# Norm sums moved to the vector engine, a reordered head of each feed-forward block, and a second queue for the last transfers, in a two-layer encoder

## The chip, the cores and the metric

The program runs on one core of a Trainium2 chip. A core has a matrix engine (PE, with its weight loads shown as PEld), a vector engine (DVE), a scalar engine (ACT), a general engine (POOL) and a sync engine (SP) that issues transfers. Each engine takes its instructions strictly in the order in which they were written for it and waits at the head of its own queue. The metric is the device time of one execution in microseconds (us); lower is better.

## The reference

A hybrid encoder of two layers over two independent sequences (256 and 512 tokens, laid side by side as 768 columns), model width 1024. What matters here, cut from the reference:

```
for l in range(DEPTH):                      # 2 layers
    mod = silu(c) @ adaln_w[l] + adaln_b[l] # shift, scale, gate, twice
    h = rmsnorm(x, norm_g[l, 0]) * (1 + sc1) + sh1
    y = mlstm_mixer(h, ...) if l == 0 else swa_mixer(h, ...)   # both end in "@ w_out"
    x = x + g1 * y
    h = rmsnorm(x, norm_g[l, 1]) * (1 + sc2) + sh2
    x = x + g2 * conv_ffn(h, ...)           # h @ w_up, conv over tokens, silu(g)*val, @ w_down
return rmsnorm(x, final_g)                  # rmsnorm: x * rsqrt(mean(x*x) + EPS) * g
```

## The kernel before, in words

**Layout.** Activations lie as 8 chunks of 128 channels (KC = 8) by tokens. Every float32 product is made of three matmuls on a high and a low part of each operand ("whi" and "wlo" for weights, "yh/yl" and "zh/zl" for activations): the cast on ACT (L260) makes the high part, a subtraction on DVE (L261) the low part. Weight loads come through a ring of five buffers called raw (issued on SP, L269).

**Output projection (`out_proj`).** The tokens are treated as two halves of 384 columns. There are 16 tiles: 8 output chunks for the first half, then 8 for the second. Each tile is 24 matmuls of 128x384 into one of four PSUM banks, then DVE adds the result to x (`resid`, L590) and ACT squares x for the coming norm (`Norm.square`, L111). `Norm.square` also adds most squares into one running sum on DVE (L115). It is a generator: `head` below runs its last part.

**The norm (`Norm`).** The mean over channels is made on PE: each kept square tile is multiplied by a constant column (tiles "pa<-inv,nt"). With `on_pe=2` three tiles are kept (one running sum and two single squares), and there are three blocks of 128 tokens, so 9 products of width 2; each shows as 2 records. Then ACT adds epsilon (L150), POOL raises to the power -1/2 (L153), and PE spreads the factor over the partitions (tiles "pa<-kct,nr"). The generator `stages` yields between these steps; `apply` then multiplies and splits. The last norm of the program has `on_pe=KC` and starts its products early (`begin`, L129).

**The head of each feed-forward block (`head`).** Pairs of up-projection chunks are computed with a seven-product scheme on quarters of h: `outset` is the first two of a chunk's products (`quarters` on B11, then on B21, 12 matmuls each, on the first half of the tokens, whose norm is done). Meanwhile the second half's norm runs, and each `step()` advances it: it makes the operands T1, T2, T4, B22 and T3 from both halves. `sums(i)` makes, on DVE and one cast on ACT, the weight combinations of chunk i of the first pair out of its raw loads. Here PE, ACT and DVE run exactly in the written order (`manual_schedule`). `mark` writes a dummy matmul into a bank to claim it. The next pairs (`pair`) make their weight combinations on POOL (L1202, L1205, L1206); `issue_after` keeps the second pair behind instructions that `head` returns.

**The end.** The last norm's `apply` is `output`: ACT copies the spread factor from PSUM to SBUF (`side`, L574); per chunk of 128x256 either DVE multiplies straight from PSUM (L581), or ACT scales (L578) and POOL multiplies by `side` (L579); each chunk goes out by a transfer on SP (L582).

Of the kernel before, what the change touches and what calls it, by code (L numbers as in the profile page):

```python
# [11 lines left out]
F32 = mybir.dt.float32  # L12
# [4 lines left out]
P = 128  # L17
# [72 lines left out]
class Norm:  # L90
# [16 lines left out]
    def square(self, c):  # L107

        net = self.net
        sq = net.tmp([P, self.n])  # L110
        net.nc.scalar.activation(sq, self.x(c), AF.Square)  # L111
        self.sums.append(sq)
        if 2 <= len(self.sums) and self.count < KC - self.on_pe:
            acc = self.sums[0]
            self.adds.tensor_tensor(acc, acc, self.sums.pop(), ALU.add)  # L115
        self.count += 1
# [3 lines left out]
    def begin(self, n):  # L120

        if self.pm is None:
            self.pm = self.net.pa()
            self.sides = [self.pm[:, 2 * b : 2 * b + 2] for b in range(self.n // P)]
            self.done = 0
        for i in range(self.done, n):
            for b, o in enumerate(self.sides):

                self.net.nc.tensor.matmul(  # L129
                    o, self.sums[i][:, b * P : (b + 1) * P], self.net.inv,  # L130
                    start=i == b == 0, stop=i == KC - 1, skip_group_check=True,
                )
        self.done = max(self.done, n)

    def stages(self):
# [17 lines left out]
        nc.gpsimd.tensor_tensor(r, r, net.mhalf[:, :nb], ALU.pow)  # L153
        yield 2.0

        pr = net.pa()[:, : self.n]
        for b in range(nb):
            net.mm(pr[:, b * P : (b + 1) * P], r[:, b : b + 1].to_broadcast([P, P]), net.ident, True, True)
# [9 lines left out]
class Net:  # L168
# [402 lines left out]
    def output(self, x, pr, rng):  # L571
        nc = self.nc
        side = self.tmp([P, rng[1] - rng[0]])
        nc.scalar.copy(side, pr)  # L574
        for c in range(KC):

            if c in ((2, 5, 7), (0, 2))[rng is RANGES[1]]:
# [4 lines left out]
            self.nc.sync.dma_start(self.io["y"][:, c, rng[0] : rng[1]], x(c))  # L582
# [9 lines left out]
    def out_proj(self, u0, act, xt, l, apply):  # L592
# [16 lines left out]
        norms = [Norm(self, xt, half, apply, last=True, adds=self.nc.vector) for half in HALVES]  # L609
# [9 lines left out]
        for i, (z, c, w) in enumerate(todo):  # L619
            if i in (KC, 2 * KC - 1):  # L620
                yield
# [452 lines left out]
    def combined(self, l, i, pool):  # L1074
# [19 lines left out]

        def apply(x, pr, rng):
            if rng[0] == 0:
                for c in range(KC):
# [9 lines left out]
            dsh = pool.tile([P, 4], F32, name="dsh")  # L1107
            nc.vector.tensor_tensor(
                dsh, self.mod[l][:, 24 * i + 4 : 24 * i + 8, q], self.mod[l][:, 24 * i : 24 * i + 4, q], ALU.subtract
            )  # L1110
# [73 lines left out]
    def outset(self, o, w, r1):  # L1184
# [3 lines left out]
        self.quarters(o, part(0), self.B11, True)  # L1188
# [68 lines left out]
    def head(self, u0, last_tile, pool, urows, mark, early):  # L1257
# [18 lines left out]
        for t in banks[0][1:]:  # L1276
            mark(t)

        def sums(i):
# [4 lines left out]
            tt(s2, s1_, s2, ALU.subtract)  # L1284
            tt(s4, s4, s2, ALU.subtract)
            tt(s1[i][1], s1_, s1[i][0].bitcast(F32), ALU.subtract)
            tt(s1_, a22, s2, ALU.subtract)

# [9 lines left out]
        sums(0)  # L1298
        wc[0] = self.split(ra[0])
# [12 lines left out]
        pa = lambda: self.pa()[:, :H]  # L1312
        second = self.outset(pa(), wa[1], rows[1][0])
        next(second)
# [54 lines left out]
        return act.ins, dve.ins  # L1369
# [298 lines left out]
```

## Time and profile before

| | |
|---|---|
| runs | 1840.19 us median of 3 (1839.05 to 1841.2) |
| the profiled execution | 1839.38 us, its span 1837.3 us |
| granted PE clock over the span | 0.993 |
| PE busy | 1792.4 us (98%) |
| DVE, ACT, POOL busy | 1373.0 (75%), 893.9 (49%), 486.6 (26%) us |
| head of layer 0 and of layer 1 | about 500 to 550 us and 1285 to 1336 us |
| last norm's spread to the end of the span | 1829.1 to 1837.3 us |

How to read it: the span runs from the first to the last instruction of the program; the execution's time has some 2 us more around it. A row of a timeline gives the start, the duration, the engine, the line, the operation with output and inputs, how many were merged (x), and in brackets how long the engine had been idle before and what ended that. Matmuls overlap: the duration of one is longer than the distance to the next one's start, and it is the distance that counts when PE is full.

### The profile page before, as it was taken

What the parts mean: (1) busy time and instruction counts of PE and PEld (TensorE: products, weight loads), DVE (VectorE), ACT (ScalarE), POOL (GpSimd) and SP (SyncE); (2) the same over time, 40 slices, a digit from 0 to 9 for tenths busy, and PEclk for the clock granted to TensorE, in tenths of its full rate; (3) what the DMA queues carried; (4) which work ended last, traced back from release to release, by engine and by line L of the source; (5) the groups of instructions that cost most, each with busy time, mean ns of one, the idle gap of its engine ahead of it and who ended that gap; (6) DMA issues with size and microseconds to landing.
All of it is one profiled execution on the core that took longest, in us unless ns stands there. A gap on an engine that the chain in (4) does not pass through costs nothing.

```text
span 1837.3 us, 28927 instructions
## 1 busy us (share of the span) xinstructions
PE 1792.4 (98%) x11290; PEld 1657.9 (90%) x11290; DVE 1373.0 (75%) x2101; ACT 893.9 (49%) x1815; POOL 486.6 (26%) x386
## 2 busy tenths in 40 slices
PE   6999999999999999999999999999999999999997
PEld 3987887889998999999999999889889999999997
DVE  4755676886689877777777867766898777787876
ACT  4444443344456444444444557665464444444443
POOL 1001001031024333333331313320234333333322
PEclk9999999999999999999999999999999999999998
DMA  8344556546312212222222331234122222222212
GB/s 332 118 147 134 172 195 223 164 140 213 104 46 71 79 58 69 69 70 69 69 69 83 114 92 42 61 97 127 46 81 70 69 69 70 70 69 70 69 35 69
DMA packets 64245, 184.48 MB, mean 100 GB/s; under 512 B 6167, under 2 KB 23831, under 8 KB 64108
## 3 DMA queue, kind: packets, MB, share of 16 engines
q1 hardware_dynamic: 64108, 182.63, 30.7%
q8 instruction: 89, 1.46, 0.3%
q14 instruction: 48, 0.39, 0.1%
HBM read 176.17 MB, written 6.43 MB: 99 GB/s over the span
## 4 chain that ended last, share of the span: by engine, by line
PE 87%; DVE 5%; DMA 3%; ACT 2%; issue 1%; POOL 1%; SPq 0%; POOLq 0%; ACTq 0%; DVEq 0%
PE ps L254 29%; PE pa L254 24%; PE ps L1169 10%; PE ps L1172 10%; PE ps L1170 10%; PE pa L1008 1%; DMA slab<-in_adaln_w_dram 1%; DMA raw<-in_adaln_w_dram 1%; DMA raw<-in_w_dram 1%; DVE wlo L261 1%; DVE ada L506 1%; PE pa L1169 0%; PE pa L1172 0%; PE pa L1170 0%; DMA slab<-mrows 0%
## 5 line engine op out<-in xcount | busy, mean ns | idle before, releaser
L260 ACT CAST whi<-raw 128x1024 fp32r<-128x1024 f32 x237 | 247.9, 1048 | 344.2 <-PE pa L254 145.6
L261 DVE TENSOR_TENSOR wlo<-raw,whi 128x1024 fp32r<-128x1024 f32 x237 | 321.7, 1358 | 112.9 <-ACT whi L260 110.5
L254 PE MATMUL pa<-slab,whi 128*128 128x256 f32 (+1 forms) x1328 | 317.2, 334 | 0.0
L254 PEld LDWEIGHTS pa<-slab,whi 128*128 128x128 f32 x1328 | 230.2, 189 | 21.8 <-DVE slab L590 0.2
L590 DVE SCALAR_TENSOR_TENSOR slab<-pa,mod,slab 128x256 f32<-128x256 f32 (+1 forms) x332 | 192.8, 598 | 65.1 <-PE pa L254 65.0
L254 PE MATMUL pa<-slab,wlo 128*128 128x256 f32 (+1 forms) x664 | 212.7, 333 | 0.0
L254 PE MATMUL ps<-zh,whi 128*128 128x256 f32 (+1 forms) x560 | 189.2, 339 | 2.2 <-ACT whi L260 1.6
L254 PE MATMUL ps<-zh,wlo 128*128 128x256 f32 (+1 forms) x560 | 183.9, 330 | 1.7 <-DVE wlo L261 1.7
L254 PE MATMUL ps<-zl,whi 128*128 128x256 f32 (+1 forms) x560 | 185.0, 333 | 0.5 <-DVE zl L552 0.5
L1169 PE MATMUL ps<-zh,whi 128*128 128x384 f32 x504 | 172.2, 342 | 3.7 <-ACT nt L1240 1.9
L1170 PE MATMUL ps<-zl,whi 128*128 128x384 f32 x504 | 169.9, 337 | 1.8 <-DVE zl L1126 1.8
L1172 PE MATMUL ps<-zh,wlo 128*128 128x384 f32 x504 | 168.9, 335 | 0.0
L254 PE MATMUL ps<-slab,whi 128*128 128x384 f32 (+2 forms) x656 | 163.1, 332 | 0.9 <-DVE slab L261 0.5
L1205 POOL TENSOR_TENSOR raw<-raw,raw 128x512 f32<-128x512 f32 x40 | 52.0, 1299 | 331.0 <-DVE wlo L261 246.4
L254 PEld LDWEIGHTS pa<-slab,wlo 128*128 128x128 f32 x664 | 125.2, 189 | 12.6 <-DVE wlo L261 0.4
L1402 POOL TENSOR_TENSOR slab<-slab 128x772 f32<-128x772 f32 x44 | 86.5, 1968 | 166.0 <-DVE slab L1390 154.0
L1389 DVE SCALAR_TENSOR_TENSOR slab<-slab,cstt,slab 128x771 f32<-128x771 f32 x88 | 104.6, 1190 | 26.7 <-ACT slab L1387 26.5
L254 PEld LDWEIGHTS ps<-zh,whi 128*128 128x128 f32 x560 | 107.4, 192 | 15.8 <-issue 4.4
L506 DVE SCALAR_TENSOR_TENSOR ada<-raw,silc,ada 128x1024 f32<-128x1024 f32 x84 | 110.2, 1350 | 14.7 <-DMA raw<-in_adaln_w_dram 14.7
L254 PEld LDWEIGHTS ps<-zl,whi 128*128 128x128 f32 x560 | 107.4, 193 | 12.7 <-issue 3.4
L1202 POOL TENSOR_TENSOR raw<-raw 128x512 f32<-128x512 f32 x40 | 65.6, 1639 | 201.0 <-DMA raw<-in_w_dram 167.8
L254 PEld LDWEIGHTS ps<-slab,whi 128*128 128x128 f32 x656 | 115.1, 188 | 3.4 <-ACT whi L260 0.9
(291 smaller groups left out, 4336.7 us busy)
## 6 DMA issues: line engine op xcount, KB each, us to landing
raw<-in_w_dram SPq DMA_DIRECT2D x208, 512.0 KB, 3.7
raw<-in_adaln_w_dram SPq DMA_DIRECT2D x84, 512.0 KB, 4.6
slab<-in_x_dram SPq DMA_DIRECT2D x12, 512.0 KB, 7.9
slab<-in_adaln_w_dram SPq DMA_DIRECT2D x12, 512.0 KB, 10.2
slab<-mrows SPq DMA_DIRECT2D x8, 384.0 KB, 5.6
xs<-slab SPq DMA_DIRECT2D x6, 512.0 KB, 3.2
bt<-brow SPq DMA_DIRECT2D x16, 192.0 KB, 3.1
slab<-xs SPq DMA_DIRECT2D x6, 512.0 KB, 5.8
```

Source lines behind the costliest of these rows:

```text
L254: self.nc.tensor.matmul(out, lhsT, rhs, start=start, stop=stop)
L260: nc.scalar.copy(hi, src)
L261: return nc.vector.tensor_tensor(lo, src, hi.bitcast(F32), ALU.subtract)
L506: stt(acc[:, s], row, w, acc[:, s], ALU.mult, ALU.add)
L590: self.nc.vector.scalar_tensor_tensor(x, o, self.mod[l][:, gc + c, q : q + 1], x, ALU.mult, ALU.add)
L1169: mm(o, wh[:, k], hi[k], start=start and k == 0, stop=False, skip_group_check=True)
L1170: mm(o, wh[:, k], lo[k], start=False, stop=False, skip_group_check=True)
L1172: mm(o, wl[:, k], hi[k], start=False, stop=k == 3, skip_group_check=True)
L1202: tt(q[2], q[2], q[3], ALU.add)
L1205: tt(q[0], q[2], q[0], ALU.subtract)
L1389: stt(y[:, 1:], u[:, :-1], w(0), y[:, 1:], ALU.mult, ALU.add)
L1402: nc.gpsimd.tensor_tensor(y, y, yrow[:, j], ALU.mult)
```

## The change

It has these parts. (1) The two norms behind the output projection get `on_pe` 0 and 1 in place of 2: more squares are added on DVE, and fewer products of width 2 are made on PE. (2) `out_proj` hands over to `head` two tiles before its end in place of one, and stops inside these two tiles, so that `head` can place their residual, square and add between its own weight sums; `begin(1)` puts the first products of the second norm right behind the last tile. (3) In `head`, the low-part matmuls of a first block stand at its end (`low`), and the norm's next step runs ahead of them; the second chunk's first block comes between the first chunk's two; chunk 1's weight cast comes behind the epsilon. (4) `head` returns the power instruction too, and the second pair's POOL work is kept behind it. (5) A small subtraction (`dsh`) moves to the first half's `apply`. (6) At the end the factor is spread twice, into two PSUM tiles (`twin`), ACT reads the second; two chunks in place of three go over ACT and POOL; transfers of chunks 1, 2, 5 and 7 are issued on ACT.

```diff
@@ Norm.square / add
-        if 2 <= len(self.sums) and self.count < KC - self.on_pe:
+        self.count += 1
+        if not self.held:
+            self.add()
+    def add(self):
+        if 2 <= len(self.sums) and self.count <= KC - self.on_pe:
             acc = self.sums[0]
             self.adds.tensor_tensor(acc, acc, self.sums.pop(), ALU.add)
-        self.count += 1
@@ Norm.stages
-        nc.gpsimd.tensor_tensor(r, r, net.mhalf[:, :nb], ALU.pow)
+        self.power = nc.gpsimd.tensor_tensor(r, r, net.mhalf[:, :nb], ALU.pow)
...
+        pr = spread()
+        net.twin = spread() if self.on_pe == KC and self.last else None
@@ output
-        nc.scalar.copy(side, pr)
+        end = rng is RANGES[-1]
+        nc.scalar.copy(side, self.twin if end else pr)
...
-            if c in ((2, 5, 7), (0, 2))[rng is RANGES[1]]:
+            turn = c in ((2, 5, 7), (0, 2), (2, 5))[2 if end else rng is RANGES[1]]
...
-            self.nc.sync.dma_start(self.io["y"][:, c, rng[0] : rng[1]], x(c))
+            queue = nc.scalar if end and c in (1, 2, 5, 7) else nc.sync
+            queue.dma_start(self.io["y"][:, c, rng[0] : rng[1]], x(c))
@@ out_proj
-        norms = [Norm(self, xt, half, apply, last=True, adds=self.nc.vector) for half in HALVES]
+        norms = [Norm(self, xt, half, apply, i, last=True, adds=self.nc.vector) for i, half in enumerate(HALVES)]
+        self.norm = norms[1]
...
+            late = i >= 2 * KC - 2
...
+            if late:
+                norms[z].held = True
+                yield
             for p0, p1, q in pieces(c0, c1):
                 self.resid(xt, o[:, p0 - c0 : p1 - c0], l, 16, c, (p0, p1, q))
             norms[z].square(c)
+            if late:
+                yield
@@ head
-        sums(0)
-        wc[0] = self.split(ra[0])
+        ops = [sums(i) for i in range(2)]
+        next(ops[0])
+        next(ops[0])
+        wc[0], low = split(ra[0])
+        next(last_tile)
+        for t in banks[0][1:]:
+            mark(t)
+        next(last_tile)
+        next(ops[0])
+        low()
+        self.norm.add()
+        next(last_tile)
+        self.norm.begin(1)
+        next(ops[1])
+        next(last_tile)
+        next(ops[1])
+        next(ops[1])
...
-        first = self.outset(fixed(0), wa[0], rows[0][0])
+        def factor():
+            step()
+            wc[1], low = split(ra[1])
+            late.append(low)
+        first = self.outset(fixed(0), wa[0], rows[0][0], factor)
         next(first)
-        step()
-        sums(1)
-        wc[1] = self.split(ra[1])
+        late.pop()()
+        second = self.outset(pa(), wa[1], rows[1][0], step)
+        next(second)
         next(first, None)
-        step()
-        second = self.outset(pa(), wa[1], rows[1][0])
-        next(second)
...
-        return act.ins, dve.ins
+        return act.ins, dve.ins, self.norm.power.ins
```

What this makes of the order of instructions, at the three places that the prediction speaks of. The line numbers of the changed kernel differ (L115 became L120, L129 L136, L150 L157, L153 L160, L254 L266, L590 L605, L1202 L1228, L1205 L1231, L1282 to L1287 L1306 to L1313).

PE, head of layer 0, from the end of the last tile of the output projection (ps_4534) to the spread of the factor; ps_4533 is chunk 0's first block, pa_5260 and pa_5232 are chunk 1's. Before, the norm's products and the blocks around them:

```order
L254 MATMUL ps_4534<-slab_3919,wlo_5133 128x384
L1169 MATMUL ps_4533<-yh,whi_5159 128x384
L1170 MATMUL ps_4533<-yl,whi_5159 128x384
L1172 MATMUL ps_4533<-yh,wlo_5160 128x384
...
L254 MATMUL pa_5213<-inv,nt_4877 128x2
L254 MATMUL pa_5213<-inv,nt_5128 128x2
L254 MATMUL pa_5213<-inv,nt_5198 128x2
...
L254 MATMUL pa_5250<-kct,nr_5223 128x128 x3
L1169 MATMUL pa_5260<-yh,zh 128x384
```

and now:

```order
L266 MATMUL ps_4534<-slab_3919,wlo_5104 128x384
L136 MATMUL pa_5196<-inv,nt_4874 128x2 x3
L1195 MATMUL ps_4533<-yh,whi_5128 128x384
L1196 MATMUL ps_4533<-yl,whi_5128 128x384
...
L136 MATMUL pa_5196<-inv,nt_5204 128x2 x3
L1202 MATMUL ps_4533<-yh,wlo_5129 128x384 x4
L1195 MATMUL pa_5232<-yh,zh 128x384
L1196 MATMUL pa_5232<-yl,zh 128x384
...
L266 MATMUL pa_5241<-kct,nr_5220 128x128 x3
L1202 MATMUL pa_5232<-yh,zl 128x384 x4
```

Nine products in one run became three at the end of the last tile and three behind eight matmuls; between the last of them and the spread lie 12 matmuls, as before. The first half's norm, earlier on PE, has 3 products in place of 9.

DVE, the same place: the weight sums of chunk 0 (raw_5116, raw_5118), the residual of the last tile but one (ps_4533) and of the last (ps_4534), and the adds of squares (nt). Before:

```order
L1282 TENSOR_TENSOR raw_5147<-raw_5147 128x512
L115 TENSOR_TENSOR nt_4877<-nt_4877,nt_5094 128x384
L590 TENSOR_SCALAR slab_4542<-ps_4533,mod_88,slab_4542 128x384
L1284 TENSOR_TENSOR raw_5145<-raw_5147,raw_5145 128x512
L1285 TENSOR_TENSOR raw_5145<-raw_5145 128x512
L1286 TENSOR_TENSOR s1l_5144<-raw_5147,s1h_5143 128x512
L1287 TENSOR_TENSOR raw_5147<-raw_5147,raw_5145 128x512
L261 TENSOR_TENSOR wlo_5170<-raw_5145,whi_5169 128x1024
L590 TENSOR_SCALAR slab_4542<-ps_4534,mod_88,slab_4542 128x384
L1282 TENSOR_TENSOR raw_5151<-raw_5151 128x512
```

and now:

```order
L120 TENSOR_TENSOR nt_4874<-nt_4874,nt_5092 128x384
L1308 TENSOR_TENSOR raw_5116<-raw_5118,raw_5116 128x512
L1310 TENSOR_TENSOR raw_5116<-raw_5116 128x512
L605 TENSOR_SCALAR slab_4542<-ps_4533,mod_88,slab_4542 128x384
L1312 TENSOR_TENSOR s1l_5115<-raw_5118,s1h_5114 128x512
L1313 TENSOR_TENSOR raw_5118<-raw_5118,raw_5116 128x512
L1320 TENSOR_TENSOR wlo_5137<-raw_5116,whi_5136 128x1024
L120 TENSOR_TENSOR nt_4874<-nt_4874,nt_5166 128x384
L1306 TENSOR_TENSOR raw_5122<-raw_5122 128x512
L1308 TENSOR_TENSOR raw_5120<-raw_5122,raw_5120 128x512
L605 TENSOR_SCALAR slab_4542<-ps_4534,mod_88,slab_4542 128x384
```

The residual of the last tile but one now stands behind two weight sums, and that of the last tile behind an add and two sums of chunk 1.

POOL, head of layer 0: the power of the second norm (nr_5223, nr_5220) and the second pair's raw sums. Before:

```order
L1202 TENSOR_TENSOR raw_5579<-raw_5579 128x512
L1380 MEMSET slab_5136 128x4x4
L1380 MEMSET slab_5137 128x4x4
L1205 TENSOR_TENSOR raw_5581<-raw_5579,raw_5581 128x512
L153 TENSOR_TENSOR nr_5223<-nr_5223,mhalf 128x3
L1206 TENSOR_TENSOR raw_5581<-raw_5581 128x512
```

and now:

```order
L1425 MEMSET slab_5107 128x4x4
L1425 MEMSET slab_5108 128x4x4
L160 TENSOR_TENSOR nr_5220<-nr_5220,mhalf 128x3
L1228 TENSOR_TENSOR raw_5573<-raw_5573 128x512
L1231 TENSOR_TENSOR raw_5575<-raw_5573,raw_5575 128x512
L1232 TENSOR_TENSOR raw_5575<-raw_5575 128x512
```

Two raw sums that stood ahead of the power stand behind it. Layer 1's head moves in the same way at all three places.

More of the change, by code (lines that the diff above doesn't have):

```diff
@@ L125, in begin @@
             self.done = 0
-        for i in range(self.done, n):
+        last = min(KC, self.on_pe + 1) - 1
+        for i in range(self.done, min(n, last + 1)):
             for b, o in enumerate(self.sides):
@@ L130, in begin @@
                     o, self.sums[i][:, b * P : (b + 1) * P], self.net.inv,
-                    start=i == b == 0, stop=i == KC - 1, skip_group_check=True,
+                    start=i == b == 0, stop=i == last, skip_group_check=True,
                 )
@@ L618, in out_proj @@
                 self.begun[i] = KC - 1
-        for i, (z, c, w) in enumerate(todo):
-            if i in (KC, 2 * KC - 1):
+        soon = []
+        for i in range(2 * KC):
+            z, c, w = soon.pop() if soon else next(todo)
+            late = i >= 2 * KC - 2
+            if i == 2 * KC - 2:
+                soon.append(next(todo))
+            if i in (KC, 2 * KC - 2):
                 yield
@@ L1093, in modulate @@
                 nc.scalar.activation(b[:, s], b[:, s], AF.Identity, bias=sh)
+        dsh = pool.tile([P, 4], F32, name="dsh")
         def apply(x, pr, rng):
             if rng[0] == 0:
+                s = self.mod[l][:, 24 * i : 24 * i + 8, 0]
+                nc.vector.tensor_tensor(dsh, s[:, 4:], s[:, :4], ALU.subtract)
                 for c in range(KC):
@@ L1182, in evict, with outset @@
             self.nc.scalar.copy(r[:, col(p0) : col(p0) + p1 - p0], o[:, p0:p1])
[L1184 removed]
+    def outset(self, o, w, r1, low=None):
         part = lambda i: [t[:, 512 * i : 512 * (i + 1)] for t in w]
[L1188 removed]
+        self.quarters(o, part(0), self.B11, True, low)
         self.nc.scalar.copy(r1[:, col(H) :], o)
```

22 lines of the change are left out of this document (12 added, 10 removed).

## The prediction

> **What bounds the kernel now.** I read the page's engine table and its chain that ended last, then the chain in order of time, then PE's timeline at the two heads and at the end.
>
> ```profile
> PE 1792.4 (98%) x11290; PEld 1657.9 (90%) x11290; DVE 1373.0 (75%) x2101; ACT 893.9 (49%) x1815; POOL 486.6 (26%) x386
> PE 87%; DVE 5%; DMA 3%; ACT 2%; issue 1%; POOL 1%; SPq 0%; POOLq 0%; ACTq 0%; DVEq 0%
> ```
>
> PE is full nearly everywhere, so two things count: matmuls taken away where PE is full, and the few places where PE waits. First the norm's products of width 2 on PE in layer 0 (first half's norm, then the second's), each run of 18 records with the row behind it:
>
> ```profile
> 476.60 2.06 PE L254 MATMUL pa<-inv,nt 128*128 128x2 f32 x18
> 478.52 0.60 PE L254 MATMUL ps<-slab,whi 128*128 128x384 f32 x2
> ...
> 511.17 2.06 PE L254 MATMUL pa<-inv,nt 128*128 128x2 f32 x18
> 513.10 0.42 PE L1169 MATMUL ps<-yh,whi 128*128 128x384 f32 x1
> 513.35 0.34 PE L1170 MATMUL ps<-yl,whi 128*128 128x384 f32 x1
> ```
>
> The runs take 1.92 us (476.60 to 478.52) and 1.93 us from start to start, 0.107 us for a record, with PE full before and after. The first wide matmul behind a run keeps PE 0.25 us (513.10 to 513.35). Then the waits for the factor, in layer 0 and in layer 1:
>
> ```profile
> 514.92 0.34 PE L1170 MATMUL ps<-yl,whi 128*128 128x384 f32 x1
> 515.09 0.34 PE L1172 MATMUL ps<-yh,wlo 128*128 128x384 f32 x1
> 515.84 0.94 PE L254 MATMUL pa<-kct,nr 128*128 128x128 f32 x6 [0.41 <-POOL nr L153]
> ...
> 1299.86 0.34 PE L1172 MATMUL ps<-yh,wlo 128*128 128x384 f32 x1
> 1301.35 0.93 PE L254 MATMUL pa<-kct,nr 128*128 128x128 f32 x6 [1.16 <-POOL nr L153]
> ```
>
> A matmul of this width normally starts 0.17 us after the last one (514.92 to 515.09). Here the next start is 0.75 and 1.49 us later, so PE loses 0.58 and 1.32 us. POOL's timeline and ACT's epsilon say why:
>
> ```profile
> 513.23 1.28 POOL L1205 TENSOR_TENSOR raw<-raw,raw 128x512 f32<-128x512 f32 x1 [5.89 <-DMA raw<-in_w_dram]
> 514.47 1.31 POOL L153 TENSOR_TENSOR nr<-nr,mhalf 128x3 f32<-128x3 f32 x1
> 515.76 2.31 POOL L1206 TENSOR_TENSOR raw<-raw 128x512 f32<-128x512 f32 x1
> ...
> 513.27 0.17 ACT L150 ACTIVATE nr<-pa 128x3 f32<-128x3 f32 x1 [1.42 <-PE pa L254]
> ...
> 1298.72 1.30 POOL L1205 TENSOR_TENSOR raw<-raw,raw 128x512 f32<-128x512 f32 x1 [6.63 <-DMA raw<-in_w_dram]
> ```
>
> The power's input is ready at 513.44, but POOL has just begun a raw sum of the second pair, which had waited for a transfer, and the power stands behind it. In layer 1 the transfer lands later in relation to the norm, so the loss is larger.
>
> **Fewer products (part 1).** Per layer 6 products leave the first norm and 3 the second: 9 products are 18 records, at 0.107 us 1.93 us, and 3.85 us over two layers. All lie on a full PE. The cover for the work that replaces them is DVE: two adds of 0.55 us (a row below) more in the first norm, one in the second. These are DVE's stretches:
>
> ```profile
> 470.00:484.00 14.00, 14.00 (x90) 14.00 (x89) 3.25 (x6) 3.29 (x6) 0.85 (x1) 1.00 0.12 37
> 484.00:515.20 31.20, 31.20 (x186) 31.11 (x185) 28.11 (x51) 19.83 (x41) 3.49 (x5) 1.00 0.27 86
> ```
>
> The third column after the length is DVE: busy 3.25 of 14 us, then 28.11 of 31.2. The two adds fit the first stretch, the third the 3 us left in the second. Without that cover the three would cost 1.65 us a layer, less than they save. The second norm's products now stand in two places, so one more switch to wide matmuls: 0.25 less 0.17, +0.08 us a layer.
>
> **The tighter order on DVE (parts 2 and 3).** PE now wants the running sum, with the last tile but one in it, right when the last tile ends. These are DVE and ACT there before, and PE's first matmul behind the last tile:
>
> ```profile
> 502.66 0.68 DVE L1282 TENSOR_TENSOR raw<-raw 128x512 f32<-128x512 f32 x1
> 503.27 0.55 DVE L115 TENSOR_TENSOR nt<-nt,nt 128x384 f32<-128x384 f32 x1
> 507.59 0.69 DVE L1287 TENSOR_TENSOR raw<-raw,raw 128x512 f32<-128x512 f32 x1
> 508.20 1.22 DVE L261 TENSOR_TENSOR wlo<-raw,whi 128x1024 fp32r<-128x1024 f32 x1
> 509.33 0.61 DVE L590 SCALAR_TENSOR_TENSOR slab<-ps,mod,slab 128x384 f32<-128x384 f32 x1
> ...
> 507.06 1.06 ACT L260 CAST whi<-raw 128x1024 fp32r<-128x1024 f32 x1 [1.14 <-DVE raw L1285]
> 509.98 0.53 ACT L111 ACTIVATE nt<-slab 128x384 f32<-128x384 f32 x1 [1.86 <-DVE slab L590]
> ...
> 509.08 0.34 PE L1169 MATMUL ps<-yh,whi 128*128 128x384 f32 x1
> ```
>
> In the new order, on the clock of before: sum at 502.66, add 503.27, then two sums of 0.69 (to 505.2), the residual 0.61 (to 505.8), two more of 0.69 (to 507.1), the low part 1.22 (to 508.2; its cast on ACT, 1.06 from 505.2, is done at 506.3), the add 0.55, done at about 508.7. PE asks at 509.08: 0.4 us to spare. Then chunk 1's two sums to 510.1, the last residual to 510.65, its square to 511.2. PE gets there after 6 records (0.64), the switch (0.08) and 8 matmuls (1.39): 511.2, a tie. I take 0.1 us of waiting a layer. Bounds: 0, and 0.6, if both sums run as slowly as a POOL operation beside them could make them (below). Queued behind a waiting PE are only the head's own blocks. The factor: epsilon 0.17 and power 1.31 after the last product end at 513.6 with hand-overs, while the 12 matmuls in between last 2.1 us, to 514.0. So the 0.58 and 1.32 us go, 1.90 together. Both ends: nothing gained, if the power comes late again, and 1.90, since no more was lost there. The marks, the reordered blocks and the changed place of the casts cost nothing: they are the same instructions, and PE did not wait for the blocks' operands before. The subtraction dsh leaves the path of the factor on DVE:
>
> ```profile
> 516.84 1.25 DVE L1108 TENSOR_TENSOR dsh<-mod 128x4 f32<-128x4 f32 x1
> ```
>
> Later PE waits for DVE again and again, from 538 to 548. Does an earlier factor help there? Rows of PE, ACT and DVE:
>
> ```profile
> 538.58 0.44 PE L1170 MATMUL ps<-bq,whi 128*128 128x384 f32 x1 [0.21 <-DVE bq L1151]
> ...
> 527.21 0.48 ACT L1189 COPY slab<-pa 128x384 f32<-128x384 f32 x1 [1.54 <-PE pa L1172]
> ...
> 530.25 0.56 DVE L1126 TENSOR_TENSOR zl<-bq,zh 128x384 fp32r<-128x384 f32 x1 [0.62 <-ACT zh L1120]
> 532.44 0.56 DVE L1126 TENSOR_TENSOR zl<-bq,zh 128x384 fp32r<-128x384 f32 x1 [1.09 <-ACT zh L1120]
> ```
>
> No: DVE idles 0.62 and 1.09 us for ACT, and ACT idled 1.54 for PE. This chain starts anew from PE at 527 to 532, behind the changed stretch. These waits stay and move with PE, so they cost and give nothing.
>
> **The end (part 6).** Rows of PE, ACT, DVE and POOL, the eight last transfers on SP, and what the DMA queue did while they ran:
>
> ```profile
> 1829.09 1.22 PE L254 MATMUL pa<-kct,nr 128*128 128x128 f32 x4 [1.04 <-POOL nr L153]
> ...
> 1830.35 0.37 ACT L574 COPY nt<-pa 128x256 f32<-128x256 f32 x1 [2.09 <-PE pa L254]
> ...
> 1830.76 2.05 DVE L581 SCALAR_TENSOR_TENSOR slab<-slab,cstt,pa 128x256 f32<-128x256 f32 x5 [5.07 <-ACT nt L574]
> ...
> 1830.80 2.09 POOL L579 TENSOR_TENSOR slab<-slab,nt 128x256 f32<-128x256 f32 x3 [1.76 <-ACT nt L574]
> ...
> 1831.26 3.79 SPq L582 DMA_DIRECT2D out_dram<-slab  x8
> ...
> q1 hardware_dynamic: 1152, 1.05, 62.9%
> ...
> DMA to landing us min/median/max: 1.7/1.8/1.8
> ```
>
> DVE waited for ACT's copy (0.41 us after ACT); it now starts at about 1830.35, and its six chunks at 0.41 each end at 1832.8, as its five did. The second spread takes PE another 0.9 to 1.2 (the first took 1.22 from 1829.09, its filling included), ACT copies 0.37 more, to 1831.6 or 1831.9, and POOL's two chunks at 0.70 are done at 1833.0 or 1833.3. Eight issues in 3.79 us (to 1835.05) put the last at about 1834.6, long after the data. ACT now issues its third when chunk 5 is ready, and the last 0.5 us later, at 1833.5 to 1833.8: 0.8 to 1.1 us earlier. The transfers kept the 16 engines busy 62.9% of the time, so there is room, but less than double. I take -1.0. Bounds: 0 if ACT issues more slowly than SP (nothing in this trace is issued there), -1.6 if nothing follows chunk 5's issue.
>
> The Trainium skill, "DMA: Bandwidth & Descriptors", section "Issuing engines are not separate DMA queues", says that issuing from more engines saves only the sequencer's time, usually small beside the transfer; by that alone the sum below would lose its 1.0. The 62.9% speaks for issue as the limit here.
>
> **The sum.** -3.85 - 1.90 + 0.16 + 0.2 - 1.0 = -6.4 us. Against the profiled execution's own 1839.38 us (span 1837.3 and about 2 around it) that is 1833.0; the median of the runs, 1840.19, lies 0.8 above that execution, so I forecast **1833.8 us**. What a measurement of this kernel can tell from no change is about 0.2%, 3.7 us.
>
> **Rivals.** *The end gives nothing*: the two queues only interleave. Then 1834.8. For it: 62.9% is not little. Against: no idle time between issues on SP.
>
> *POOL holds DVE up.* The raw sums now run while DVE makes chunk 1's sums and the first operands. Against running side by side: dsh, four columns wide, took 1.25 us and ended at 518.09, when POOL's L1206 (515.76 and 2.31) ended. Two sums of 1.28 and one of 2.31 could hold DVE for 4.9 us in each head. Its cover is dsh's 1.25 and the idle 0.62 and 1.09: 3.0. The rest, 1.9 a layer, PE would wait: 1837.6. Against: the operations alternate, and POOL can be the one that waits. The Trainium skill, "SBUF — State Buffer", section "SBUF: two separate sides", has the same as a rule: a vector operation with two SBUF inputs and a POOL operation exclude each other, the later waiting for the whole of the earlier. The dsh row agrees.
>
> *PE absorbs it*: the waits from 538 on hang on something that does not move with PE, and swallow the heads' 5.4 us. Only the end is left: 1839.2. Against it stand ACT's and DVE's idle rows.
>
> *Slower: ACT's queue.* The page's list of issues shows SP alone. The slowest kind in the page:
>
> ```profile
> slab<-in_adaln_w_dram SPq DMA_DIRECT2D x12, 512.0 KB, 10.2
> ```
>
> If the last transfer took 10.2 us from its issue at 1833.5, it would land at 1843.7. Before, the last landed at 1834.6 and 1.8, 1836.4. That is +7.3 against the heads' -5.4: 1842.1. It decides from a landing time of some 8.3 us. Against: these transfers are 128 KB, and those 512 KB in a crowd.
>
> **How the numbers follow.** Forecast 0.62, end gives nothing 0.13, POOL holds DVE up 0.12, absorbed 0.07, ACT's queue 0.06. Faster by over 0.2% means under 1836.5: the first two and a little of the third, 0.78. Within 0.2%: 0.16. Slower: 0.06. The range of 1831.0 to 1837.6 holds the forecast with its unknowns (down: the end's -1.6, no waits on DVE, and a run as low as 1839.05 was to the median; up: 0.6 of waiting a layer, nothing at the end) and reaches to the held-up DVE; it leaves out 0.13 and a rest.
>
> **What would show it.** Right: runs of 6 records in place of 18; the power on POOL before both raw sums, no wait of PE at the spread in either head; DVE's last multiplies starting within 0.1 us of the first spread; the last output landing about 1 us sooner behind the spread. Wrong: a wait of PE over 0.3 us for the running sum or the last square, DVE operations stretched beside POOL's raw sums with PE waiting more than before at 527 to 548, or a transfer on ACT that lands later than 2 us after its issue.

## The result, and the profile after

The changed kernel took 1832.56 us, the median of five runs (1830.30 to 1834.59), beside 1839.05 us for the kernel before (1836.62 to 1841.20, five runs): ratio 0.9964, 95% interval [0.9953, 0.9976]. The profiled execution took 1832.56 us, its span 1830.8 us, 6.5 us less than before's. The forecast was 1833.8 us, in a range of 1831.0 to 1837.6. The total came as forecast. Its parts did not all.

From the page of the changed kernel, its engines and the chain that ended last:

```profile
PE 1789.2 (98%) x11258; PEld 1653.6 (90%) x11258; DVE 1379.1 (75%) x2108; ACT 893.0 (49%) x1814; POOL 483.8 (26%) x385
PE 85%; DVE 5%; issue 4%; ACT 3%; DMA 1%; POOL 1%; SPq 0%; POOLq 0%; ACTq 0%; DVEq 0%
```

PE has 32 records less: 36 fewer of the norms' products, 4 more of the second spread. PE's timeline in the head of layer 0, then of layer 1:

```profile
509.85 0.78 PE L136 MATMUL pa<-inv,nt 128*128 128x2 f32 x6
510.49 0.42 PE L1195 MATMUL ps<-yh,whi 128*128 128x384 f32 x1
...
512.21 0.83 PE L136 MATMUL pa<-inv,nt 128*128 128x2 f32 x6
...
514.89 0.34 PE L1196 MATMUL pa<-yl,zh 128*128 128x384 f32 x1
515.07 0.83 PE L266 MATMUL pa<-kct,nr 128*128 128x128 f32 x6
...
1296.41 0.34 PE L1196 MATMUL pa<-yl,zh 128*128 128x384 f32 x1
1296.58 0.83 PE L266 MATMUL pa<-kct,nr 128*128 128x128 f32 x6
```

Two runs of 6 records stand where 18 stood, and the spread starts 0.18 and 0.17 us behind the start of the matmul ahead of it: no wait there in either head. POOL and DVE in layer 0's head:

```profile
513.33 0.90 POOL L160 TENSOR_TENSOR nr<-nr,mhalf 128x3 f32<-128x3 f32 x1 [5.23 <-ACT nr L157]
514.20 1.28 POOL L1228 TENSOR_TENSOR raw<-raw 128x512 f32<-128x512 f32 x1
515.57 2.15 POOL L1231 TENSOR_TENSOR raw<-raw,raw 128x512 f32<-128x512 f32 x1
...
514.25 2.33 DVE L1320 TENSOR_TENSOR wlo<-raw,whi 128x1024 fp32r<-128x1024 f32 x1 [0.72 <-ACT whi L1319]
516.50 0.60 DVE L1139 SCALAR_TENSOR_TENSOR slab<-slab,gain,pa 128x384 f32<-128x384 f32 x1
```

The power runs ahead of the raw sums. Chunk 1's low part on DVE takes 2.33 us beside them (1.22 before), but the first multiply by the factor still starts 1.4 us behind the spread. The end:

```profile
1823.71 2.07 PE L266 MATMUL pa<-kct,nr 128*128 128x128 f32 x8 [1.03 <-POOL nr L160]
1824.96 2.44 DVE L595 SCALAR_TENSOR_TENSOR slab<-slab,cstt,pa 128x256 f32<-128x256 f32 x6 [4.66 <-PE pa L266]
1825.47 2.11 SPq L597 DMA_DIRECT2D out_dram<-slab  x4
1825.82 0.37 ACT L587 COPY nt<-pa 128x256 f32<-128x256 f32 x1 [2.94 <-PE pa L266]
1825.88 2.67 ACTq L597 DMA_DIRECT2D out_dram<-slab  x4
1826.27 1.41 POOL L593 TENSOR_TENSOR slab<-slab,nt 128x256 f32<-128x256 f32 x2 [2.61 <-ACT nt L587]
```

From the spread to the end it is 7.1 us; before, it was 8.2.

**Where the 6.5 us lie.** Two executions don't start alike, so I compare stage by stage. For each ACT and DVE instruction that stands in both traces I take its start here less its start before; the difference of two such offsets (medians over a short stretch) is what a stage gained. Two pairs of rows as an example, the same square on ACT ahead of layer 0's head (before, then after), and the first products of layer 1's mixer (before, then after):

```profile
464.93 0.52 ACT L111 ACTIVATE nt<-slab 128x384 f32<-128x384 f32 x1 [2.91 <-DVE slab L590]
467.06 0.52 ACT L111 ACTIVATE nt<-slab 128x384 f32<-128x384 f32 x1 [2.18 <-DVE slab L605]
1021.50 0.72 PE L254 MATMUL pa<-inv,nt 128*128 128x2 f32 x6
1020.20 0.50 PE L266 MATMUL pa<-inv,nt 128*128 128x2 f32 x4
```

The changed kernel came 2.13 us later to its first head, and 1.30 us earlier to the mixer. Heads are 465 to 555 us and 1230 to 1365 us, bodies the rest of each feed-forward block (585 to 960 and 1400 to 1780 us). "Late" is from there to the last spread. All against the profiled execution of before, in us:

```
kernel              start  head 0  body 0  head 1  body 1   late    end   whole
after               +2.12   -2.35   -1.03   -2.83   -1.24  -0.01  -1.11   -6.49
before_addr         +4.18   +0.02   -1.07   -0.56   -1.27  +0.54  +0.01   +1.79
after_addr_back     +1.15   -2.28   +0.16   -3.88   -0.13  +1.80  -1.11   -4.26
after_split_place   +2.83   -2.33   -0.18   -3.98   -0.52  +0.44  -1.12   -4.86
after_yh            +2.34   -2.25   -1.10   -3.88   -1.38  +1.24  -1.11   -6.23
before_tail         +1.59   +0.12   -0.06   -1.67   -0.14  +1.92  -1.12   +0.63
before_sums         +2.16   -1.64   +0.17   -3.21   -0.14  -0.48   0.00   -3.10
before_power        +1.20   +1.27   +0.01   -0.49    0.00  +1.47   0.00   +3.48
before_both         +1.84   -0.77    0.00   -2.45   +0.01  +0.02  -0.01   -1.34
after_no_power      +0.90   +2.58   -1.06   -0.68   -1.25  +0.04  -1.11   -0.64
after_all_sp        +2.43   -2.35   -1.10   -3.98   -1.26  -0.48  -0.40   -7.19
after_dsh_late      +1.55   -2.36   -0.85   -3.98   -1.24  +2.26  -1.11   -5.77
after_yh_sp7        +0.74   -2.32   -1.48   -2.84   -1.38  -0.15  -1.17   -8.73
```

(Layer 1's mixer, left out, moves by 0.13 at most.) Three columns hold chance. *Start*: every other execution came to the heads 0.7 to 4.2 us later than the profiled one of before, the unchanged code of before_tail among them. *Late*: before_tail lost 1.92 us there, in code that nobody touched; there PE's granted clock falls to a half before the program ends, and in before_tail it fell sooner (a mean of 0.61 in its 6 us ahead of 1823.6, against 0.94 in 1816 to 1822 of before). *Head 1*: the old order costs 1.67 us less in before_tail than in the profiled run of before, which waits 1.16 us at the spread (before_tail 0.62) and 0.97 us at 1332 (before_tail not at all). So a head in layer 1 is read against before_tail's where it has no such wait at 1332: the changed order then gains 2.2 to 2.3 there (-3.88 to -3.98, less -1.67), as in layer 0.

Head 0, head 1 and the end were forecast. The two bodies, 2.27 us, were not.

### The profile page after: what moved, and what is told of

Same layout as the page of the kernel before. It is cut to its first block, busy times and chain, and to the rows that moved or that the text cites. A ratio compares the mean times of both kernels' runs of the same rounds, so it can differ in the third digit from the quotient of the medians.

```text
span 1830.8 us, 28867 instructions
## 1 busy us (share of the span) xinstructions
PE 1789.2 (98%) x11258; PEld 1653.6 (90%) x11258; DVE 1379.1 (75%) x2108; ACT 893.0 (49%) x1814; POOL 483.8 (26%) x385
## 4 chain that ended last, share of the span: by engine, by line
PE 85%; DVE 5%; issue 4%; ACT 3%; DMA 1%; POOL 1%; SPq 0%; POOLq 0%; ACTq 0%; DVEq 0%
PE ps L266 27%; PE pa L266 24%; PE ps L1195 10%; PE ps L1196 10%; PE ps L1198 10%; PE pa L1034 1%; DVE wlo L273 1%; DMA slab<-in_adaln_w_dram 0%; DMA raw<-in_adaln_w_dram 0%; PE pa L1195 0%; PE pa L1196 0%; DVE ada L518 0%; ACT whi L272 0%; PE pa L1198 0%; ACT zh L1146 0%
## 5 line engine op out<-in xcount | busy, mean ns | idle before, releaser
L272 ACT CAST whi<-raw 128x1024 fp32r<-128x1024 f32 x233 | 243.8, 1049 | 332.5 <-PE pa L266 145.0
L273 DVE TENSOR_TENSOR wlo<-raw,whi 128x1024 fp32r<-128x1024 f32 x233 | 316.7, 1360 | 105.6 <-ACT whi L272 103.5
L266 PE MATMUL pa<-slab,whi 128*128 128x256 f32 (+1 forms) x1328 | 317.3, 334 | 0.0
L266 PEld LDWEIGHTS pa<-slab,whi 128*128 128x128 f32 x1328 | 230.1, 189 | 21.9 <-DVE slab L605 0.4
L605 DVE SCALAR_TENSOR_TENSOR slab<-pa,mod,slab 128x256 f32<-128x256 f32 (+1 forms) x332 | 192.7, 598 | 63.8 <-PE pa L266 63.6
L266 PE MATMUL pa<-slab,wlo 128*128 128x256 f32 (+1 forms) x664 | 212.8, 333 | 1.4 <-DVE wlo L273 1.4
L266 PE MATMUL ps<-zh,whi 128*128 128x256 f32 (+1 forms) x560 | 189.3, 339 | 2.6 <-ACT whi L272 1.9
L266 PE MATMUL ps<-zh,wlo 128*128 128x256 f32 (+1 forms) x560 | 184.1, 331 | 2.0 <-DVE wlo L273 2.0
L266 PE MATMUL ps<-zl,whi 128*128 128x256 f32 (+1 forms) x560 | 184.5, 332 | 0.5 <-DVE zl L564 0.5
L266 PE MATMUL ps<-slab,whi 128*128 128x384 f32 (+2 forms) x656 | 163.5, 332 | 0.9 <-DVE slab L273 0.5
L266 PEld LDWEIGHTS pa<-slab,wlo 128*128 128x128 f32 x664 | 125.2, 189 | 14.3 <-DVE wlo L273 2.0
L1231 POOL TENSOR_TENSOR raw<-raw,raw 128x512 f32<-128x512 f32 x40 | 53.7, 1343 | 318.5 <-DVE wlo L273 245.8
L1434 DVE SCALAR_TENSOR_TENSOR slab<-slab,cstt,slab 128x771 f32<-128x771 f32 x88 | 108.9, 1239 | 26.7 <-ACT slab L1432 26.4
L266 PEld LDWEIGHTS ps<-zh,whi 128*128 128x128 f32 x560 | 107.6, 192 | 16.1 <-issue 4.4
L266 PEld LDWEIGHTS ps<-zl,whi 128*128 128x128 f32 x560 | 107.3, 192 | 12.6 <-issue 3.4
L266 PEld LDWEIGHTS ps<-slab,whi 128*128 128x128 f32 x656 | 115.2, 188 | 3.4 <-ACT whi L272 0.9
L266 PEld LDWEIGHTS ps<-zh,wlo 128*128 128x128 f32 x560 | 107.1, 192 | 12.2 <-DVE wlo L273 2.9
```

The source lines that it names most:

```text
L266: self.nc.tensor.matmul(out, lhsT, rhs, start=start, stop=stop)
L272: nc.scalar.copy(hi, src)
L273: return nc.vector.tensor_tensor(lo, src, hi.bitcast(F32), ALU.subtract)
L605: self.nc.vector.scalar_tensor_tensor(x, o, self.mod[l][:, gc + c, q : q + 1], x, ALU.mult, ALU.add)
L1231: tt(q[0], q[2], q[0], ALU.subtract)
L1434: stt(y[:, 1:], u[:, :-1], w(0), y[:, 1:], ALU.mult, ALU.add)
```

## Experiments

**1. A tile's place in memory.** In the bodies PE never waits longer than before, but matmuls on bq, s1h and s1l follow each other faster. Part 5 also moves the place of dsh: it is now allocated first, and 32 bytes further on lie bq, s1h and s1l (bq from byte 212928 of the partition to 212960, s1h from 225216 to 225248, in the built program). Three kernels change that place alone:

```diff
# before_addr: before, the tile made first, its instruction unmoved
+            self.dsh = pool.tile([P, 4], F32, name="dsh")   # behind yh, yl
-            dsh = pool.tile([P, 4], F32, name="dsh")
+            dsh = self.dsh
# after_addr_back: the changed kernel, the other tiles' places claimed first
+        one(F32)
+        for t in ("s1h", "s1l"):
+            pool.tile([P, 512], R, tag=t, name=self.nm(t), bufs=1)
         dsh = pool.tile([P, 4], F32, name="dsh")
# after_split_place: the same with one(F32) alone
```

> The kernel before, with one thing changed: the small tile dsh (32 bytes a partition) takes its place in memory ahead of the tiles bq, s1h and s1l, as in the changed kernel, so these lie 32 bytes further on (bq from byte 212928 to 212960). Every instruction stands where it stood. Theory 'place': the distance between matmuls that read bq or s1h/s1l falls from about 176.5 to about 173.7 ns as in the changed kernel, some 500 a layer, so each feed-forward body (600 to 1000 us, and 1370 to 1800 us) is shorter by about 1.1 us and the whole by about 2.2 us: ratio 0.9988. Theory 'order': the drift in the bodies comes from the reordered heads and what they trigger; then nothing changes here, 176.5 ns stays, ratio 1.0000.

> The changed kernel with dsh's place in memory behind s1l, as before, so bq, s1h and s1l lie on their old bytes; instructions in the changed order. Theory 'place': 173.7 ns goes back to about 176.5 ns at bq and s1h/s1l, the two bodies are longer by about 1.1 us each, and of the gain of 6.5 us about 4.3 are left: ratio to before 0.9976. Theory 'order': all stays, ratio 0.9964.

> The changed kernel with dsh's place between bq and s1h: bq on its old bytes (212928), s1h and s1l 32 bytes further on (225248). If the place of the streamed tile and that of the weights count each for its own matmuls: bq back to about 176 ns, s1h/s1l stay at 174.0 ns, and each body gives back about half, 0.5 to 0.6 us. If only one of the two counts: both numbers move together with that one.

Measured: before_addr 1837.68 us, ratio 0.9987 [0.9978, 0.9995]; after_addr_back 1833.44 us, 0.9960 [0.9948, 0.9972]; after_split_place 1834.21 us (one run). The times alone can't tell after_addr_back from the changed kernel, and the 0.9976 that "place" named for it lies outside its interval; the stages can tell. The bodies gain 1.07 and 1.27 us in before_addr, nothing in after_addr_back (+0.16, -0.13), and half as much or less in after_split_place (-0.18, -0.52). The groups of PE by form show it, with the mean duration behind the busy time; before, after, before_addr and after_split_place, a row on bq and one on s1h each:

```profile
L1169 PE MATMUL ps<-bq,whi 128*128 128x384 f32 x168 | 57.2, 341 | 0.0
L1169 PE MATMUL ps<-zh,s1h 128*128 128x384 f32 x160 | 54.2, 339 | 0.0
...
L1195 PE MATMUL ps<-bq,whi 128*128 128x384 f32 x168 | 56.5, 336 | 0.0
L1195 PE MATMUL ps<-zh,s1h 128*128 128x384 f32 x160 | 53.8, 336 | 0.0
...
L1169 PE MATMUL ps<-bq,whi 128*128 128x384 f32 x168 | 56.5, 336 | 0.0
L1169 PE MATMUL ps<-zh,s1h 128*128 128x384 f32 x160 | 53.8, 336 | 0.0
...
L1196 PE MATMUL ps<-bq,whi 128*128 128x384 f32 x168 | 57.1, 340 | 0.0
L1196 PE MATMUL ps<-zh,s1h 128*128 128x384 f32 x160 | 53.8, 336 | 0.0
```

Where PE is full the distance from start to start counts (mean of those under 200 ns, both layers):

```
ns                  bq (524)   s1h, s1l (498)   yh, yl (904)   zh, zl on whi, wlo (1527)
before               176.24        176.57          175.95           174.19
after                173.85        174.01          175.50           174.30
before_addr          173.86        174.01          175.51           174.36
after_addr_back      175.94        176.58          175.92           174.18
after_split_place    175.79        173.99          175.57           174.43
after_yh             173.86        174.03          174.32           174.73
```

2.39 ns on 524 and 2.56 on 498 are 2.5 us. The place theory holds, and each operand counts for its own matmuls, the streamed one (bq) and the weights (s1h). The order of the heads has no part in it: before_addr has the old order and the gain, after_addr_back the new order and no gain. Why the place counts is not shown.

**2. The same for two more tiles.** In after_yh dsh is made ahead of yh and yl, so that these lie 32 bytes further on too.

> The changed kernel with dsh's place ahead of yh and yl as well, so that these too lie 32 bytes further on (188352 to 188384) with bq and s1h/s1l where the changed kernel has them. Instructions unchanged. Theory 'place', if it holds for any tile that PE reads: the about 450 matmuls a layer on yh and yl go from 175.5 to about 174 ns, 0.7 to 0.9 us a layer, 1.4 to 1.8 us in all: ratio to before 0.9955. Theory 'order', or a place that matters for bq and s1 alone: as the changed kernel, 0.9964.

1832.82 us, 0.9955 [0.9943, 0.9967]. yh and yl fell by 1.2 ns, 1.1 us in all, but zh and zl rose by 0.43 ns on 1527 matmuls, 0.65 us. The bodies gain 0.07 and 0.14 us on the changed kernel: nearly nothing. That the ratio is the 0.9955 that "place" named is luck: it stood for 1.4 to 1.8 us. So the place matters for more than one pair of tiles, but zh and zl, which did not move, became slower at the same time; why is open.

**3. Parts 1 and 4 on their own.** before_sums has only `on_pe` 0 and 1, before_power only the power among the instructions that hold the second pair back, before_both these two; after_no_power is the changed kernel without that one.

```diff
# before_sums
+        norms = [Norm(self, xt, half, apply, i, last=True, ...) for i, half in enumerate(HALVES)]
# before_power (after_no_power takes the same away)
-        return act.ins, dve.ins
+        return act.ins, dve.ins, self.norm.power.ins
```

> The kernel before with part 1 alone (on_pe 0 and 1: 6 records of width 2 in the first norm, 12 in the second, in the old order). Theory 'additive': 18 records less a layer at 0.107 us, head of layer 0 and of layer 1 each shorter by 1.9 us, the wait at the spread as before (0.5 to 1.2 us): ratio 0.9979. Theory 'pinned': the power stands behind a raw sum on POOL that starts when a transfer lands, so the 0.64 us of the second norm, or all of it, only lengthens the wait at the spread: heads shorter by 0.7 to 1.3 us, the wait at the spread longer by 0.6 or more: ratio 0.9989.

> The kernel before with one line of part 4 alone: the second pair's POOL work is kept behind the power. Theory: PE's wait at the spread goes in both heads, 0.6 us in layer 0 and 0.8 us in layer 1 (1.3 in the profiled run of before), 1.4 to 1.9 us in all, nothing comes back at 530 to 550 us: ratio 0.9991. Rival 'POOL holds DVE up': the raw sums, now later, run beside the operands that DVE makes, and PE waits more at 530 to 575 us by as much as it gained: ratio 1.0000.

> The kernel before with parts 1 (sums) and 4 (power) and nothing else: old order of DVE and PE in the heads, dsh and the tail as before. If parts 2 and 3 only make room and give nothing themselves: heads shorter by 2.3 to 2.6 us each, as in the changed kernel (2.3): ratio 0.9974. If the new order of DVE is needed (the add of the last square but one stands ahead of the weight sums here, and DVE waits for ACT there): PE waits for chunk 0's low part or for the last square, and the heads are shorter by 1.5 to 2.0 us each: ratio 0.9981.

> The changed kernel without the power in the list that holds the second pair's POOL work back. If the hold is what takes away the wait: PE waits at the spread again, 0.6 us or more in each head, since the products now end earlier while the raw sum starts when its transfer lands: 1.4 to 3.0 us lost of the gain, ratio to before 0.9975. If the other order alone already brings the power ahead: as the changed kernel, 0.9963.

Measured: before_sums 1836.25 us, 0.9980 [0.9971, 0.9989]; before_power 1842.86 us, 1.0016 [1.0007, 1.0025], slower than before; before_both 1838.58 us, 0.9995 [0.9986, 1.0003]; after_no_power 1840.08 us, 1.0005 [0.9995, 1.0014]. Together, without parts 2 and 3, parts 1 and 4 gain 0.77 us in head 0 and 0.78 in head 1 (-2.45 against before_tail's -1.67), a third of the changed kernel's. The timelines of POOL, DVE, ACT and PE in before_power say why:

```profile
514.73 0.85 POOL L153 TENSOR_TENSOR nr<-nr,mhalf 128x3 f32<-128x3 f32 x1 [6.19 <-ACT nr L150]
515.54 1.48 POOL L1203 TENSOR_TENSOR raw<-raw 128x512 f32<-128x512 f32 x1
...
515.91 1.66 DVE L1288 TENSOR_TENSOR raw<-raw,raw 128x512 f32<-128x512 f32 x1
517.50 2.31 DVE L261 TENSOR_TENSOR wlo<-raw,whi 128x1024 fp32r<-128x1024 f32 x1
519.73 1.25 DVE L1109 TENSOR_TENSOR dsh<-mod 128x4 f32<-128x4 f32 x1
520.90 0.60 DVE L1114 SCALAR_TENSOR_TENSOR slab<-slab,gain,pa 128x384 f32<-128x384 f32 x1
...
522.18 0.51 ACT L1121 CAST zh<-bq 128x384 fp32r<-128x384 f32 x1 [4.98 <-DVE bq L1131]
522.60 0.47 ACT L1190 COPY slab<-pa 128x384 f32<-128x384 f32 x1
...
521.12 0.34 PE L1173 MATMUL pa<-yh,zl 128*128 128x384 f32 x1
523.12 0.44 PE L1170 MATMUL pa<-yh,zh 128*128 128x384 f32 x1 [1.67 <-ACT slab L1190]
```

The power is early and the wait at the spread is gone. But in the old order chunk 1's last sum and low part still lie ahead of DVE, and now run beside POOL's raw sums: 1.66 us in place of 0.69 and 2.31 in place of 1.22. The first multiply starts at 520.90, 4.4 us behind the spread (516.46). ACT's cast waits for it, and ACT's copy that empties a PSUM bank stands behind that cast. PE waits 1.67 us for the bank, 2.00 from start to start where 0.17 is normal. That is the rival "POOL holds DVE up", 1.8 us a head; less the 0.58 that the early power saves, head 0 is 1.27 us longer. before_both has the same 1.67 in both heads. before_sums has such a wait too, 0.68 us; the power happens to be ready ahead of the raw sum there, so "pinned" is wrong, and "additive" meets the ratio but not the heads (1.9 us each, with the wait at the spread). In the changed kernel chunk 1's sums, with their cast on ACT, stand ahead of the epsilon, and the multiply comes in time. dsh, 1.25 us, lies on this path too; to move it alone in the old order was not tried.

Without the hold in the new order, rows of DVE, POOL and PE in layer 0, PE's in layer 1, and stretches with the granted clock (PEclk, the number behind POOL's), two of layer 0 and one of layer 1:

```profile
505.50 1.26 DVE L1312 TENSOR_TENSOR s1l<-raw,s1h 128x512 fp32r<-128x512 f32 x1
...
512.36 1.67 POOL L1231 TENSOR_TENSOR raw<-raw,raw 128x512 f32<-128x512 f32 x1 [5.49 <-DMA raw<-in_w_dram]
514.11 2.12 POOL L1232 TENSOR_TENSOR raw<-raw 128x512 f32<-128x512 f32 x1
516.19 0.86 POOL L160 TENSOR_TENSOR nr<-nr,mhalf 128x3 f32<-128x3 f32 x1
...
509.14 0.83 PE L136 MATMUL pa<-inv,nt 128*128 128x2 f32 x6 [0.36 <-DVE nt L120]
...
517.10 1.04 PE L266 MATMUL pa<-kct,nr 128*128 128x128 f32 x6 [2.52 <-POOL nr L160]
...
519.54 0.52 PE L1196 MATMUL ps<-yl,whi 128*128 128x384 f32 x1
519.86 0.52 PE L1198 MATMUL ps<-yh,wlo 128*128 128x384 f32 x1
...
1303.49 0.93 PE L266 MATMUL pa<-kct,nr 128*128 128x128 f32 x6 [2.53 <-POOL nr L160]
...
1305.14 0.34 PE L1196 MATMUL ps<-yl,whi 128*128 128x384 f32 x1
1305.32 0.34 PE L1198 MATMUL ps<-yh,wlo 128*128 128x384 f32 x1
...
517.00:519.00 2.00, 1.90 (x10) 1.90 (x11) 0.78 (x2) 0.00 (x0) 0.16 (x2) 0.70 0.46 170
519.00:521.30 2.30, 2.30 (x9) 2.30 (x8) 2.26 (x4) 0.90 (x2) 1.58 (x1) 0.52 0.00 0
1304.00:1306.00 2.00, 2.00 (x14) 2.00 (x14) 1.50 (x3) 0.23 (x1) 0.58 (x1) 1.00 0.22 90
```

The power now stands behind two raw sums, and PE waits 2.52 us at the spread in head 0 and 2.53 in head 1. In head 0 it comes back at about half clock: matmuls 0.32 us apart (519.54 to 519.86) until 521.1, which costs 1.6 us more. In head 1, after the same wait, the clock stays at 1.00 and the matmuls stand 0.17 to 0.18 us apart. A raw sum on POOL also runs beside DVE earlier (one of DVE's sums takes 1.26 us in place of 0.68), and PE waits 0.36 and 0.57 us for the running sum. So the hold is worth 4.9 us in head 0 (+2.58 against -2.35), more than the whole change gained there, and 3.3 in head 1 (-0.68 against -3.98).

**4. dsh on DVE's path.** The subtraction back at its old place on DVE, its memory at the new one.

```diff
# after_dsh_late, in the second half's apply; taken out of the first half's
+            nc.vector.tensor_tensor(dsh, ...mod[l][:, 24*i+4 : 24*i+8, q], ...mod[l][:, 24*i : 24*i+4, q], ALU.subtract)
```

> The changed kernel with the subtraction dsh at its old place on DVE, behind the spread; its place in memory stays the new one. If dsh was a cost on the path from the factor to the first operand (1.25 us for four columns, beside a POOL operation): the first multiply comes 0.8 to 1.3 us later, ACT's copies that free a PSUM bank stand behind it, and PE waits at chunk 1's second block or the third block, 0.3 to 1.2 us a head. As the prediction had it (nothing waits there, later waits start anew from PE): heads shorter by 2.3 us as in the changed kernel, no new wait.

1831.94 us, 0.9952 [0.9936, 0.9968]; heads as in the changed kernel (-2.36 and -3.98), no new wait. As an instruction part 5 gives nothing in the new order: the first multiply comes 2.6 us behind the spread in place of 1.4, and nothing waits for it. It is the place of its tile that gives 2.3 us.

**5. The end.** before_tail is before with part 6; after_all_sp is the changed kernel with all transfers on SP; after_yh_sp7 is after_yh with chunk 7's on SP.

```diff
# after_all_sp, then after_yh_sp7
-            queue = nc.scalar if end and c in (1, 2, 5, 7) else nc.sync
+            queue = nc.sync
+            queue = nc.scalar if end and c in (1, 2, 5) else nc.sync
```

> The kernel before with part 6 alone (factor spread twice, two chunks over ACT and POOL, transfers of chunks 1, 2, 5, 7 issued on ACT). As forecast: DVE starts 0.4 us earlier, the last issue comes 0.8 to 1.1 us earlier behind the spread, the span from the last spread to the end falls from 8.2 to about 7.1 us: -1.0 us, ratio 0.9994. Rival 'interleave': the two queues share one throughput, the end stays at 8.2 us: ratio 1.0000.

> The changed kernel with all last transfers on SP; the second spread and two chunks over ACT and POOL stay. If issue is the limit: 8 issues at 0.47 us start 0.4 us sooner behind the spread than before, since DVE starts 0.4 us sooner, and the last comes 0.4 us sooner: spread to end 7.8 us (before 8.2, changed 7.1). If the second queue gives nothing by itself: 7.1 us. If the early start gives nothing: 8.2 us. In all cases the heads as in the changed kernel.

> The changed kernel with yh and yl moved by 32 bytes too and chunk 7's transfer back on SP. ACT's last issue, chunk 7's, came at 4.4 us behind the spread, because chunk 5's stood ahead of it and waited for POOL until 4.0 us; SP was done with its fourth issue at 3.9. With chunk 7 as SP's fifth the last issue comes at about 4.0 us, spread to end 6.7 us: 0.4 us off, and 0.2 us off in the bodies: 0.6 us under the changed kernel, ratio to before 0.9960. Rival: SP's issue of chunk 7 and ACT's of chunk 5 only swap places, 7.1 us.

before_tail: 1839.35 us, 0.9995 [0.9986, 1.0004], too little for the times to tell, but its end is 1.12 us shorter. after_all_sp: 1832.18 us, 0.9957 [0.9943, 0.9971]; end 0.40 us shorter. after_yh_sp7: 1830.51 us, 0.9948 [0.9935, 0.9961]. Behind the last spread, in the traces:

```
us                 first issue   last issue   end of span   from last issue to end
before                 2.17          5.55         8.17             2.62
after_all_sp           1.77          5.15         7.77             2.62
after, before_tail     1.77          4.43         7.06             2.63
after_yh_sp7           1.77          4.00         7.01             3.01
```

The second spread, with one chunk less on POOL, gives 0.40 us, the second queue 0.71. Chunk 7 on SP brings the last issue 0.43 us forward as expected, but the end only 0.05: the two last transfers now start together (3.97 on SP and 4.00 on ACT). ACT's lands at 5.93, SP's has no record, and the span ends at 7.01. So 0.4 was wrong, and the last issue no longer sets the end; what does stays open. Summed over the bodies and the end this kernel is 0.65 us under the changed one; the intervals of the times overlap.

## Why the prediction was right, and where not

**Fewer products, -3.85.** Right in size where nothing else comes late. Head 0 is 2.35 us shorter; 18 records at 0.107 and the 0.58 at the spread are 2.51, less 0.08 for the switch and 0.09 of waiting. But it was not the products alone: before_sums gained 1.64 and 1.54 (-3.21 against -1.67), with a new wait of 0.68 us.

**The power ahead, -1.90.** The wait went in both heads. Its size was that of one execution: PE was idle 0.41 and 1.16 us there, 0.51 and 0.62 in before_tail, 0.47 and 0.66 in before_addr. With 0.17 for each that is 1.90, 1.47 and 1.47 us. The term was 0.4 too large for a usual run.

**"The marks, the reordered blocks and the changed place of the casts cost nothing."** They cost nothing, and this step still missed their worth. The sum treated parts 1 and 4 as gains of their own; they are not. before_power was slower than before, and before_both gained a third. Chunk 1's sums ahead of the epsilon (part 2) and the new order of casts and blocks (part 3) together keep DVE in time: before_both lacks them and waits, after_dsh_late has them without part 5's early dsh and does not. Which of the two weighs more was not tried. The rival that I gave 0.12 is real, and the order that I called neutral kept it away. One sign that I named for it came even so: DVE's low part takes 2.33 us beside the raw sums. But PE's waits from 527 to 548 are the same as before. The Trainium skill's rule in "SBUF — State Buffer", section "SBUF: two separate sides", fits the rows: DVE's operations with two SBUF inputs stretch by about 1.0 to 1.1 us beside POOL's raw sums.

**Waiting for the running sum and the last square, +0.2.** Right: PE is idle 0.09 us at the second products of head 0 and 0.02 in head 1, and no time at the first. The tie was one. The bound of 0.6 was no idle one: without the hold PE waits 0.36 and 0.57 us at the first. The waits from 538 on did move with PE, as said.

**The end, -1.0.** Right: -1.11 and -1.12, DVE started 1.25 us behind the spread (1.67 before), and ACT's transfers land as fast as SP's (1.7 to 1.9 us). The rule in the Trainium skill, "DMA: Bandwidth & Descriptors", section "Issuing engines are not separate DMA queues", names what was gained, the sequencer's time; here that was 0.71 of 7.8 us.

**What no step had: the bodies, -2.27.** I costed dsh's move as an instruction and never asked where its tile lies. Neither the diff nor the order of instructions shows it. The typical sum is then -2.35 -2.25 -2.27 -1.11, about -8.0 us, inside the measured interval of -4.4 to -8.6 (ratio 0.9976 to 0.9953). The profiled run shows -6.5 since it started 2.1 us late and before's head 1 was a dear one (-2.83 in place of -2.25). So the total agreed partly because an unseen gain met an oversized term and chance.

## What to carry to other kernels

Moving work ahead in one queue (the power on POOL) pays only if the work that then runs beside it (DVE's sums) is out of the way; cost such parts together, not one by one. When a tile is allocated earlier or later, all tiles behind it in the pool move: compare their bytes, and the distance between matmuls per tile, before giving a gain to the schedule. A difference of a few tenths of a per cent is read from stage lengths of two traces, with the unchanged stages as the measure of chance.

## What the hardware showed

- A shift of 32 bytes in a partition, from a multiple of 64 to 32 past one, took 2.4 to 2.6 ns off the distance between 128x384 matmuls (176.2 to 173.9 for the streamed tile, 176.6 to 174.0 for the weights). zh, zl, whi and wlo all lie 32 past a multiple of 64. Whether that is the rule or the place relative to other tiles isn't settled: yh and yl on a multiple of 64 ran at 173.5 to 174.4 ns in the heads, with weights kept in zh and zl, and moving yh and yl slowed zh and zl by 0.4 ns.
- After 2.52 us of idle time PE came back at half clock, until 4 us behind the end of the wait (after_no_power, head 0); after 2.53 us in head 1 of the same run, and after 1.67 us in before_power, it came back at 0.17 us a matmul. So the length of the wait alone doesn't decide it here. The Trainium skill, "TensorE: Matmul & The Clock Gate", section "What's actually happening", puts the fall behind an idle window of about 3.4 us. Here it came sooner, in one head of two.
- Eight transfers were issued within 2.66 us on SP and ACT together (1.77 to 4.43 us behind the spread), within 3.38 us on SP alone (1.77 to 5.15), and each still landed 1.7 to 1.9 us after its issue where that is recorded.
